# One step of a hybrid RG-LRU and GLA layer: smaller blocks in the order of the work, and a weight load in four pieces

## Chip, cores and metric

The kernel runs on one core of one Trainium2 chip. The metric is the device time of one execution in microseconds, lower being better. The core's engines each work through a queue of their own: TensorE (PE in the profile, with its weight loads as PEld), VectorE (DVE), ScalarE (ACT), GpSimd (POOL) and SyncE (SP), which here does little but issue DMA transfers. They wait for one another through semaphores, so an instruction that must wait holds up everything behind it on its engine.

## The reference

One layer of a decoder, for a prompt of 2048 tokens and 8 single-token samples, all in float32, width 1024:

```
ada = silu(c) @ w_ada + b_ada;  shift, scale, gate = split(ada)
hn = rmsnorm(x, g_norm) * (1 + scale) + shift
xa, za, q, k, v, glr, zg = split(hn @ w_in)
xc = conv_b + 4-tap causal conv of xa
gx, ga = sigmoid(xc @ w_gate_x + b), sigmoid(xc @ w_gate_a + b)   # 8 diagonal blocks of 128
log_a = 8 * ga * log_sigmoid(lambda);  a = exp(log_a)
h_t = a_t * h_{t-1} + sqrt(1 - exp(2 log_a)) * gx * xc;  y_lru = h * silu(za)
log_alpha = log_sigmoid(glr @ w_gla_g2 + b) / 16
S_t = diag(alpha_t) S_{t-1} + k_t^T v_t;  o_t = q_t S_t           # 4 heads, dk 128, dv 256
y_gla = rmsnorm(o) * g * silu(zg)
x = x + gate * (concat(y_lru, y_gla) @ w_out);  y = rmsnorm(x, g_final)
```

The outputs are y and the new states, for the prompt and for the samples.

## The kernel before, in words

**Precision and tiles.** Every float32 operand of a matmul is split into a high part (a rounded copy, made by ScalarE, `S.copy`) and a low part (what is left, by VectorE, `V.tensor_tensor(... subtract)`). A product is three matmuls, high by high, high by low and low by high, added in one PSUM bank. There are four banks tagged `acc`, two tagged `tp` (for turns, that is transposes through TensorE, and for some products), and one each tagged `kv` and `o`.

**Stages.** The prompt is worked in two halves of 1024 tokens. In each half come first the four GLA heads in the order 3, 0, 1, 2 (`gla_head`): projections of q, k and v (L396 to L398, L702 to L704), the decay (L852 to L866, L940 to L977), and the chunks of the linear attention (L1014 to L1053), whose output is turned and written to DRAM. Then come the `couples`: pairs of column blocks of the input projection for the RG-LRU and for zg, each by a Strassen-Winograd scheme of seven products (`Couple.product`, L1549) in place of eight. In the second half the split weights of these products are read back from DRAM (`wtd`), where the first half put them. The output projection follows, 16 `Pair`s of token tiles by the same scheme (L2117).

**What sets the order.** A function that is due later is put in a heap by `after(units, fn)`. `tick(0.5)` moves the clock after each half of a projection (24 matmuls, in bursts of three) and after each product of a couple (12 matmuls, 2.72 us in the chain of waits), and calls what has come due. So one unit is some 5.4 us. A scheduler then orders the instructions of each engine by readiness, but a block under `with behind(V)` is tied behind the last VectorE instruction written before it (L718), and so for S and SP.

**The pieces that the change touches.**

- `second_rows` (L1311 to L1352) makes the inputs of the second half during the first: `load` brings in two x tiles by SyncE (L1314), `norm` squares them on ScalarE (L228), `scale` takes the inverse root of the mean squares (`scales`, 12 small VectorE instructions, L163 to L169) and multiplies two tiles by it (`times`, L244), and `step` turns them (L255) in four steps, writing sums for the Winograd scheme with GpSimd (L1338 to L1342). The x buffers come free with the last turn.
- `sample_out` (to L1107) norms a head's output for the samples in the same way; its turn is L1131, and what it makes is added at L1134.
- `gla_turn` (L1109) turns a head's output of 512 tokens, 128 values at a time: four transposes into a `tp` bank (L1113), twice. `keep` copies the bank to `ob` (L1220, ScalarE) and stores that to `od` in DRAM (L1221, issued by ScalarE). `ob` has `half + 1` buffers: one in the first half. For the last head `gate` multiplies in place instead (L1227). `finish` (L1231) calls it.
- `out_weights(f, ...)` (L773) multiplies the output weights by the gate vector and makes their Winograd sums, a half of the rows in each of two calls, f=0 during the heads of the second half and f=1 during its couples. `begin(q)` loads the gate and its bias `bt` (L779, L780); `add` adds them (L785); `step` does one of four pairs of row tiles for each of two column halves: a product with the gate (L806), four differences (L810 to L813), a high and a low part (L828), stores to `wd` and `wd2`, and the load of the next tile (L795).
- `low_op(..., units)` (L1903) loads a token operand of the couples from `fd` (L1298) and splits it (`split_op`, L1305 and L1306) so many units later. S1 and S2 are two of these operands.
- `Couple.prepare` splits the weights of a product (L1495, L1496), and `combine` forms the weight sums (L1529 to L1531) on GpSimd. For the first four products of a half's first couple this happens at once (`now`); for others by `after`.
- `Lru.gates` (L1674) makes the two gate products of a 512-token segment: `xh`, `xl` are the high and low part of the convolution's output (L1671, L1672), `wgh`, `wgl` those of the gate weights. Two gates, each three matmuls in the order wgh xh, wgh xl, wgl xh (L1682 to L1684), then a tanh (L1685).
- The weights of the first output product, B11, are 2 MB, both parts already made (`wd2`). `early_w` loads them (L1924) in the last couples, at the product that the table `at` of the `couples` call names: (10, 0) is the first product of couple 10. `early_rows` (L1943) loads and splits the first token operands of the output projection in the same stretch.

## Time and profile before

| | |
|---|---|
| median of 3 runs | 1478.83 us (1476.04 to 1481.50) |
| the profiled execution | 1481.88 us, of which its span is 1480.1 us |
| mean granted TensorE clock | 0.988 |
| instructions in the span | 22516 |
| DMA, mean over the span | 231 GB/s |
| first half: heads, then couples | to about 343 us, to about 611 us |
| second half: heads, then couples | to about 893 us, to about 1148 us |
| output projection, and its end | to about 1466 us, to 1480 us |

Times inside the span are counted from its first instruction. A row of the timeline has the start, the duration, the engine, the line, the operation, what it writes and reads, and in brackets the idle time of the engine before it with what ended that. A row of a list of waits has who waited, for what, the total, how often, and the longest. The chain of waits follows the work that ended last back to its start. A queue's name with a q (SPq, ACTq) is an engine's instruction that issues a transfer or handles a semaphore. The granted clock is the share of TensorE's full clock that the chip allowed.

### The profile page before, as it was taken

To read this page: it belongs to the slowest core of one execution; us is meant where nothing else is said; L and a number is where in the kernel's file an instruction comes from. 1 tells how busy PE (TensorE), PEld (TensorE's weight loads), DVE (VectorE), ACT (ScalarE), POOL (GpSimd) and SP (SyncE) were. 2 spreads that over 40 slices of the span, in tenths; PEclk is the share of its full clock that TensorE was granted. 3 is DMA by queue.
4 is the path that set the end of the run, shared out by engine and by line. 5 is a ranking of instruction groups with operands and counts; after the bars stand their busy time and mean duration, and the time that the engine had idled before them with its cause. 6 is when DMAs were issued, how large, how long until landed. Compare 5 with 4: busy or idle time off the path is not lost.

```text
span 1480.1 us, 22516 instructions
## 1 busy us (share of the span) xinstructions
PE 1417.9 (96%) x8113; PEld 1172.7 (79%) x8113; DVE 1098.0 (74%) x2402; ACT 699.0 (47%) x1310; POOL 212.2 (14%) x258
## 2 busy tenths in 40 slices
PE   8999998899999999889899999999999999999997
PEld 6888978787777777779798888778777787777786
DVE  5767975658788888756767864788866886688886
ACT  4634353544675767333433532666563532144332
POOL 0200154334313222001111100000002000000000
PEclk9999999999999999999999999999999999999999
DMA  9725665536778558973857536798889867694352
GB/s 322 263 87 191 220 231 191 206 142 222 273 257 289 190 181 288 341 252 136 287 171 275 172 107 225 277 296 290 290 260 371 326 212 271 231 354 141 133 174 100
DMA packets 172436, 341.89 MB, mean 231 GB/s; under 512 B 12418, under 2 KB 101794, under 8 KB 168605
## 3 DMA queue, kind: packets, MB, share of 16 engines
q1 hardware_dynamic: 136325, 277.92, 55.1%
q0 software_dynamic: 13392, 46.54, 8.0%
q10 hardware_dynamic: 22608, 15.99, 3.3%
q8 instruction: 64, 1.05, 0.3%
q14 instruction: 47, 0.39, 0.1%
HBM read 205.78 MB, written 134.69 MB: 230 GB/s over the span
## 4 chain that ended last, share of the span: by engine, by line
PE 52%; DVE 15%; DMA 9%; ACT 5%; issue 4%; SPq 0%; ACTq 0%; DVEq 0%
PE acc L2117 11%; PE tp L2117 8%; PE acc L1549 6%; PE tp L1549 4%; PE acc L704 3%; PE acc L702 3%; PE acc L703 3%; DVE tg L1700 2%; PE acc L396 2%; PE acc L397 2%; PE acc L398 2%; DMA raw<-in_w_in_dram 1%; DVE op L1496 1%; DVE cv L1667 1%; DVE tx L1698 1%
## 5 line engine op out<-in xcount | busy, mean ns | idle before, releaser
L1549 PE MATMUL acc<-op,op 128*128 128x512 f32 x1056 | 252.3, 393 | 6.1 <-DMA op<-wtd 3.6
L1549 PEld LDWEIGHTS acc<-op,op 128*128 128x128 f32 x1056 | 198.2, 189 | 49.5 <-DMA op<-wtd 4.0
L1549 PE MATMUL tp<-op,op 128*128 128x512 f32 x792 | 196.1, 393 | 2.3 <-DVE acc L1559 2.3
L2117 PE MATMUL acc<-w,a 128*128 128x512 f32 (+1 forms) x792 | 187.2, 389 | 1.8 <-DVE w L1982 1.8
L2117 PEld LDWEIGHTS acc<-w,a 128*128 128x128 f32 x792 | 146.7, 188 | 37.6 <-issue 3.4
L1549 PEld LDWEIGHTS tp<-op,op 128*128 128x128 f32 x792 | 146.9, 188 | 34.4 <-DVE acc L1559 3.2
L396 PE MATMUL acc<-w,op 128*128 128x256 f32 (+1 forms) x508 | 151.9, 299 | 2.0 <-ACT w L374 1.2
L397 PE MATMUL acc<-w,op 128*128 128x256 f32 (+1 forms) x508 | 145.4, 286 | 0.4 <-DVE w L375 0.4
L398 PE MATMUL acc<-w,op 128*128 128x256 f32 (+1 forms) x508 | 145.5, 286 | 0.2 <-DVE op L271 0.2
L2117 PE MATMUL tp<-w,a 128*128 128x512 f32 x564 | 137.2, 393 | 0.0
L2117 PEld LDWEIGHTS tp<-w,a 128*128 128x128 f32 x564 | 105.2, 188 | 27.9 <-issue 5.2
L702 PE MATMUL acc<-op,w 128*128 128x512 f32 x296 | 121.9, 412 | 0.3 <-ACT w L374 0.3
L704 PE MATMUL acc<-op,w 128*128 128x512 f32 x296 | 117.0, 395 | 0.0
L703 PE MATMUL acc<-op,w 128*128 128x512 f32 x296 | 116.5, 394 | 0.0
L396 PEld LDWEIGHTS acc<-w,op 128*128 128x128 f32 x508 | 98.0, 193 | 4.2 <-ACT w L374 1.6
L397 PEld LDWEIGHTS acc<-w,op 128*128 128x128 f32 x508 | 97.3, 192 | 1.5 <-DVE w L375 0.6
L398 PEld LDWEIGHTS acc<-w,op 128*128 128x128 f32 x508 | 97.2, 191 | 0.6 <-DVE op L271 0.4
L1979 ACT CAST a<-s 128x512 fp32r<-128x512 f32 x61 | 36.5, 619 | 102.9 <-issue 35.6
L228 ACT ACTIVATE junk<-on 128x256 bf16<-128x256 f32 x64 | 26.7, 417 | 113.1 <-DVE on L1053 95.1
L1667 DVE SCALAR_TENSOR_TENSOR cv<-xa,vecT,cv 128x512 f32<-128x512 f32 x96 | 72.8, 758 | 5.8 <-ACT cv L1665 5.1
L1049 DVE TENSOR_TENSOR states<-states,pkv 128x256 f32<-128x256 f32 x60 | 25.0, 417 | 58.3 <-PE po L1048 58.0
L704 PEld LDWEIGHTS acc<-op,w 128*128 128x128 f32 x296 | 55.9, 189 | 12.2 <-DVE w L375 0.2
(442 smaller groups left out, 2833.3 us busy)
## 6 DMA issues: line engine op xcount, KB each, us to landing
wtd<-op SPq DMA_DIRECT2D x77, 512.0 KB
op<-wtd SPq DMA_DIRECT2D x77, 512.0 KB
w<-parts SPq DMA_DIRECT2D x16, 1024.0 KB
a<-mixd SPq DMA_DIRECT2D x63, 256.0 KB
parts<-w POOLq DMA_DIRECT2D x12, 1024.0 KB, 5.9
w<-wd SPq DMA_DIRECT2D x10, 1024.0 KB
wr<-in_w_in_dram SPq DMA_DIRECT2D x18, 512.0 KB
wada<-in_w_ada_dram SPq DMA_DIRECT2D x16, 512.0 KB
```

The lines of the kernel that those rows point to most:

```text
L228: S.activation(junk[:m, :n], x, AF.Square, accum_out=out)
L396: PE.matmul(ps, part(0, kt, c), hi[:, kt % 4], start=kt == 0, stop=False)
L397: PE.matmul(ps, part(0, kt, c), lo[:, kt % 4], start=False, stop=False)
L398: PE.matmul(ps, part(1, kt, c), hi[:, kt % 4], start=False, stop=kt == KT - 1)
L702: PE.matmul(ps[:, :n], hi[:, kt], a, start=kt == 0, stop=False)
L703: PE.matmul(ps[:, :n], hi[:, kt], b, start=False, stop=False)
L704: PE.matmul(ps[:, :n], lo[:, kt], a, start=False, stop=kt == KT - 1)
L1549: PE.matmul(ps, w[:, u, k], t[:, v, k], start=q < 3 and (k, u, v) == (0, 0, 0), stop=(k, u) == (3, 1), skip_group_check=True)
L1667: V.scalar_tensor_tensor(cv, xa[:, k:k + 512], cw[k], cv, op0=OP.mult, op1=OP.add)
L1700: V.tensor_tensor_scan(h, a, tx, 0.0 if self.half == 0 else hc[:, j:j + 1], op0=OP.mult, op1=OP.add)
L1979: S.copy(t[:, 0, k], (low(t) if src is None else src)[:, k])
L2117: PE.matmul(ps, t[:, u, k], w[:, v, k, c], start=(q < 3 or ps is own) and (k, u, v) == (0, 0, 0), stop=(k, u) == (3, 1), skip_group_check= ...
```

## The change

Eight edits, none of which changes a matmul's count:

1. `second_rows.scale` and `sample_out.scale` leave the inverse root to the scheduler; only the multiplication is tied behind VectorE, and in `second_rows` it comes half a unit later.
2. `gla_turn` takes a `gap`. For the first three heads of the first half the second turn comes one unit after the first.
3. The first couple's `combine` runs on VectorE instead of GpSimd. The later couples keep GpSimd.
4. The gate products are ordered wgh xh and wgl xh for both gates, then wgh xl for both with the tanh behind each. The two gates' banks are open together.
5. `out_weights(0)` begins after 2.5 units in place of 0.5, and its bias is added after 2 units in place of 1.5; for f=1 after 1 in place of 1.5.
6. The operands S1 and S2 of the second half are split 3 units after their load is issued, in place of 2.
7. B11's 2 MB load becomes four of 512 KB, a row tile each, behind the products (10, 0), (9, 5), (9, 6) and (10, 2). In the order of the products these come in turn.
8. `early_rows` loads its second operand a unit after the first and splits it 3.5 units in, in place of 3.

```diff
--- before.py
+++ after.py
@@ -785,7 +785,7 @@
                     V.tensor_tensor(g, g, bt, op=OP.add)
                 step(q, 0, r, g)

-            after(1.5, add)
+            after(2 - f, add)

         def load(q, m):
             r = hp.tile([P, 2, 2, 256], F32, tag="r", name="r", bufs=2)
@@ -1099,19 +1099,24 @@
         square_sum(xp, ss[:, :1], os_, P, DV)

         def scale():
+            rsqrt(gp, rs[:, :1], ss[:, :1], 1, P, 1.0 / DV)
             with behind(V):
-                rsqrt(gp, rs[:, :1], ss[:, :1], 1, P, 1.0 / DV)
                 V.tensor_scalar(os_, os_, rs[:, :1], None, op0=OP.mult)
         after(0.5, scale)
         after(2.5, done, True)
         more()

-    def gla_turn(h, s, on, done):
-        for dt in range(2):
+    def gla_turn(h, s, on, done, gap=0):
+        def one(dt):
             pt = tps()
             for c in range(4):
                 PE.transpose(pt[:, c * P:(c + 1) * P], on[:, c, dt * P:(dt + 1) * P], ident)
             done(2 * h + dt, dt, pt)
+        one(0)
+        if gap:
+            after(gap, lambda: one(1), True)
+        else:
+            one(1)

     def silu(z, src):
         log_exp[0] = False
@@ -1232,7 +1237,7 @@
             if final and (s, 1) not in zs:
                 after(0.5, lambda: finish(s), True)
                 return
-            gla_turn(h, s, prep[s, "run"][1], gate(s) if final else keep(s))
+            gla_turn(h, s, prep[s, "run"][1], gate(s) if final else keep(s), 0 if final or half else 1)

         pk = None
         if not wv:
@@ -1320,9 +1325,13 @@
             after(0.5, lambda: scale(p, x, ss))

         def scale(p, x, ss):
-            with behind(V):
-                times(x, scales(xp, ss, 2))
-            after(1, lambda: step(p, x, 0))
+            rs = scales(xp, ss, 2)
+
+            def mult():
+                with behind(V):
+                    times(x, rs)
+                after(1, lambda: step(p, x, 0))
+            after(0.5, mult)

         def step(p, x, k):
             if p == 0 and not ready:
@@ -1500,7 +1509,7 @@
             if q == B11:
                 self.slot(q)
                 split(q, b11)
-                (self.combine if now else lambda: after(self.wait, self.combine))()
+                (lambda: self.combine(V)) () if now else after(self.wait, self.combine)
             elif q == T2:
                 self.slot(q)
                 if now:
@@ -1515,7 +1524,7 @@
                 self.slot(q)
                 split(q, {B21: b21, T3: b12, B22: b22, T4: b11}[q])

-        def combine(self):
+        def combine(self, q=G):
             r = self.raw
             b11, b12, b21, b22 = [r[:, 4 * k:4 * k + 4, b] for k in range(2) for b in range(2)]
             if self.half == 0:
@@ -1526,9 +1535,9 @@
                 sample_cols(lambda kt: r[:, kt].rearrange("p b n -> p (b n)"), 2 * P,
                             [(zsam[:, n], 1.0) for n in self.sam], tmp, acc, self.wait)
             t = self.t2 = lp.tile([P, 4, P], F32, tag="t2", name="t2")
-            G.tensor_tensor(b11, b12, b11, op=OP.subtract)
-            G.tensor_tensor(t, b22, b11, op=OP.subtract)
-            G.tensor_tensor(b12, b22, b12, op=OP.subtract)
+            q.tensor_tensor(b11, b12, b11, op=OP.subtract)
+            q.tensor_tensor(t, b22, b11, op=OP.subtract)
+            q.tensor_tensor(b12, b22, b12, op=OP.subtract)

         keep, wait, more = None, 0.75, ()

@@ -1677,11 +1686,14 @@
                 self.tx, self.tg = self.t_("tx"), self.t_("tg")
             tx, tg = self.tx, self.tg
             c = slice(SEGS[s][0], SEGS[s][0] + 512)
+            both = []
             for g, (out, bias) in enumerate(((tx, hbx), (tg, hba))):
                 ps = gps()
+                both.append((ps, out, bias))
                 PE.matmul(ps, wgh[:, g], xh, start=True, stop=False)
-                PE.matmul(ps, wgh[:, g], xl, start=False, stop=False)
-                PE.matmul(ps, wgl[:, g], xh, start=False, stop=True)
+                PE.matmul(ps, wgl[:, g], xh, start=False, stop=False)
+            for g, (ps, out, bias) in enumerate(both):
+                PE.matmul(ps, wgh[:, g], xl, start=False, stop=True)
                 S.activation(out[:, c], ps, AF.Tanh, bias=bias[:, j:j + 1], scale=0.5)
             if s == 0:
                 return
@@ -1894,13 +1906,13 @@
     after(5, samples_silu)
     owp = gpx.enter_context(tc.tile_pool(name="owp", bufs=1, side="right"))
     ow = Scratch(6)
-    after(0.5, lambda: out_weights(0, ow, owp, lambda: ow.tile([P, 2, 256], F32, tag="g"), lambda: low_op(1, S1, fd[4], units=2)))
+    after(2.5, lambda: out_weights(0, ow, owp, lambda: ow.tile([P, 2, 256], F32, tag="g"), lambda: low_op(1, S1, fd[4], units=3)))
     scs.append(Scratch(3))
     log_exp[0] = False
     for k, h in enumerate(HEADS):
         w = gla_head(1, h, k, w=w)
         if k == 1:
-            low_op(1, S2, fd[5], units=2)
+            low_op(1, S2, fd[5], units=3)
     flush()
     samples_conv()
     gpx.close()
@@ -1925,10 +1937,11 @@
         else:
             SP.dma_start(low(w), wd[f, WD[q]])

-    def early_w(q, place):
+    def early_w(k):
         def load():
-            with behind(SP):
-                load_w(0, q, place)
+            if k == 0:
+                wts[0, B11] = ops.tile([P, 2, 4, 512], F32R, tag="o0", name="w")
+            low_dma(wts[0, B11][:, :, k].bitcast(F32), wd2[0, :, :, k])
         return load

     def open_pre():
@@ -1943,9 +1956,11 @@

         r = [lp.tile([P, TH], F32, tag=tag, name="r").rearrange("p (q k t) -> p q k t", q=2, k=4) for tag in ("tx", "a")]
         lo = [early[n][:, 1].bitcast(F32) for n in range(2)]
-        for n in range(2):
+        def load(n):
             low_dma(lo[n], mixd[2 * n, :, :4])
             low_dma(r[n], mixd[2 * n + 1, :, :8].rearrange("p (q k) t -> p q k t", q=2))
+        load(0)
+        after(1, lambda: load(1))

         def add(n):
             with behind(S), behind(V):
@@ -1961,7 +1976,7 @@
                 V.tensor_tensor(early[2 + n][:, 1], r[n][:, 0], early[2 + n][:, 0].bitcast(F32), op=OP.subtract)

         after(2, lambda: add(0))
-        after(3, lambda: add(1))
+        after(3.5, lambda: add(1))

     open_s()
     done = []
@@ -1969,7 +1984,7 @@
     end = Zg(1, HEADS[2])
     end.more = [lambda: am.rearrange("p c t -> p (c t)")]
     couples([Lru(1, j) for j in range(KT)] + [Zg(1, h) for h in HEADS[:2]] + [end], at={(0, 0): lambda: low_op(1, S4, fd[7]),
-                                                (0, 6): lambda: low_dma(o[4][0, 0, HEADS[3]], St[HEADS[3]]), (9, 2): open_pre, (10, 0): early_w(B11, 0)})
+                                                (0, 6): lambda: low_dma(o[4][0, 0, HEADS[3]], St[HEADS[3]]), (9, 2): open_pre, (10, 0): early_w(0), (9, 5): early_w(1), (9, 6): early_w(2), (10, 2): early_w(3)})
     flush()
     sx.close()
```

How the order moves is shown at three places. The first is VectorE at the start of the second half's first head. `L785` adds the bias; `L852` to `L854` split the decay's low-rank input `g`, `L866` copies its turn, `L910` is the low part of the values, `L884` copies the samples' values. Before:

```order
L910 TENSOR_TENSOR vl<-acc,vh 128x256
L785 TENSOR_TENSOR scratch<-scratch,bt 128x512
L884 COPY vs<-acc 8x68
L806 TENSOR_TENSOR scratch<-scratch 128x512
L884 COPY vs<-acc 8x68
L806 TENSOR_TENSOR scratch<-scratch 128x512
L852 CAST g_6513<-acc 8x16
L853 CAST g_6513<-acc 8x16
L854 TENSOR_TENSOR g_6513<-acc,g_6513 8x16
```

After, some twenty rows further on in the same queue:

```order
L866 CAST gls<-tp 48x512
L910 TENSOR_TENSOR vl<-acc,vh 128x256
L852 CAST g_6583<-acc 128x16
L853 CAST g_6583<-acc 128x16
L854 TENSOR_TENSOR g_6583<-acc,g_6583 128x16
L910 TENSOR_TENSOR vl<-acc,vh 128x256
L852 CAST g_6616<-acc 128x16
L853 CAST g_6616<-acc 128x16
L854 TENSOR_TENSOR g_6616<-acc,g_6616 128x16
L785 TENSOR_TENSOR scratch<-scratch,bt 128x512
L806 TENSOR_TENSOR scratch<-scratch 128x512 x2
L866 CAST gls<-tp 48x512
```

The add and the two products with the gate have moved from ahead of the samples' copies and the last five splits of g to behind them all, in front of the second large copy L866.

The second place is VectorE between the second and the third head of the second half, around the split of the operand S2 (`op_7653` before, `op_7640` after). `L1262` (L1267 after) finishes the scaled keys that TensorE turns at L1014; `L1018` masks the attention products. Before:

```order
L1306 TENSOR_TENSOR op_7653<-op_7653 128x1024
L168 SCALAR_TENSOR_TENSOR rs_t<-rs_t,rs_x 128x1
L951 TENSOR_TENSOR xb<-xb,e 128x8
L1306 TENSOR_TENSOR op_7653<-op_7653 128x1024
L169 SCALAR_TENSOR_TENSOR ors_7451<-rs_t,rs_y 128x1
L1271 TENSOR_TENSOR e<-acc,e 128x512
L1104 TENSOR_SCALAR os<-os,ors_7451 128x256
L1262 SCALAR_TENSOR_TENSOR xb<-acc,xb 128x512
L785 TENSOR_TENSOR scratch<-scratch,bt 128x512
```

After, where L1267 stands eleven rows ahead of the first of these:

```order
L1018 COPY_PREDICATED am<-mask,tp 128x512
L1024 TENSOR_TENSOR kTl<-tp,kTh 128x512
L1021 TENSOR_TENSOR aml<-am,amh 128x512
L1277 SCALAR_TENSOR_TENSOR xb<-acc,xb 128x512
L1139 SCALAR_TENSOR_TENSOR mixs<-tp,gsc,zsam 128x8 x2
L1049 TENSOR_TENSOR states<-states,pkv 128x256
L1053 COPY on<-po 128x256
L1050 TENSOR_SCALAR states<-states,f 128x256
L1049 TENSOR_TENSOR states<-states,pkv 128x256
L1053 COPY on<-po 128x256
L1050 TENSOR_SCALAR states<-states,f 128x256
L1311 TENSOR_TENSOR op_7640<-op_7640 128x1024 x2
```

The split (L1311 after) has moved from ahead of the keys to behind the mask and two state updates L1049.

The third place is TensorE among the last heads of the first half (near 290 us in the profile), at the turns of one head's output; `op_146`, `op_147` and so on are the token operands of a value projection that runs there. Before:

```order
L704 MATMUL acc<-op_146,w 128x512
L1113 MATMUL tp<-ident,on 128x128 x4
L702 MATMUL acc<-op_147,w 128x512
L703 MATMUL acc<-op_147,w 128x512
L1113 MATMUL tp<-ident,on 128x128 x4
L704 MATMUL acc<-op_147,w 128x512
```

After, the second of the two turns:

```order
L255 MATMUL tp<-ident,scratch 128x128 x4
L704 MATMUL acc<-op_148,w 128x512
L1113 MATMUL tp<-ident,on 128x128 x4
L702 MATMUL acc<-op_149,w 128x512
L703 MATMUL acc<-op_149,w 128x512
L1014 MATMUL tp<-xb,e 128x128 x4
L1017 MATMUL tp<-ident,e 128x128 x4
```

The first turn stays ahead of op_147; the second has moved thirteen matmuls of the projection further, to two matmuls ahead of the L1014 and L1017 that come next.

## The prediction

> **What bounds the kernel now.** I read the page's busy times first, then the list of what TensorE waited for.
>
> ```profile
> PE 1417.9 (96%) x8113; PEld 1172.7 (79%) x8113; DVE 1098.0 (74%) x2402; ACT 699.0 (47%) x1310; POOL 212.2 (14%) x258
> ```
>
> TensorE is busy for 1417.9 of the span's 1480.1 us, and no edit removes a matmul. All that can be won lies in the remaining 62 us and in stretches at a lower clock. The list of TensorE's waits (total, times, longest) names the idle time that the eight edits touch:
>
> ```profile
> PE tp L1014 <- DVE xb L1262: 5.3, 1, 5.3
> PE tp L255 <- DVE am L1018: 4.3, 1, 4.3
> PE tp L1014 <- ACT ob L1220: 3.7, 1, 3.7
> PE tp L864 <- DVE g L854: 3.6, 1, 3.6
> PE acc L1549 <- DMA op<-wtd: 3.6, 1, 3.6
> PE gps L1682 <- ACT xh L1671: 3.6, 5, 1.3
> PE gps L1683 <- DVE xa L1657: 2.7, 4, 0.7
> PE acc L1549 <- DVE op L1496: 2.5, 1, 2.5
> PE gps L1683 <- DVE xl L1672: 1.5, 3, 0.7
> PE tp L1131 <- DVE f L967: 0.9, 1, 0.9
> ```
>
> Five are single waits of 3.6 to 5.3 us. What follows each is in a table of stretches (length; busy time and count of PE, weight loads, DVE, ACT, POOL; granted clock; DMA share; GB/s):
>
> ```profile
> 228.00:232.00 4.00, 3.93 (x21) 3.93 (x22) 2.61 (x6) 1.77 (x4) 2.20 (x5) 0.57 0.71 281
> 290.00:297.00 7.00, 6.26 (x23) 5.58 (x24) 2.12 (x3) 3.89 (x7) 3.83 (x7) 0.51 0.32 115
> 349.00:356.00 7.00, 6.90 (x43) 4.95 (x44) 6.46 (x11) 2.87 (x4) 1.97 (x2) 1.00 0.95 358
> 635.00:642.00 7.00, 6.39 (x30) 6.31 (x31) 3.19 (x16) 0.98 (x3) 1.52 (x2) 0.53 0.70 166
> 734.00:738.00 4.00, 3.84 (x17) 3.69 (x18) 3.96 (x13) 0.81 (x2) 0.00 (x0) 0.60 0.03 12
> 1130.00:1135.00 5.00, 2.03 (x5) 1.65 (x6) 2.62 (x5) 0.71 (x2) 0.18 (x1) 0.81 1.03 409
> 1135.00:1140.00 5.00, 5.00 (x20) 4.01 (x20) 2.59 (x4) 0.59 (x1) 0.75 (x1) 0.85 1.06 422
> ```
>
> Behind each of the five the granted clock is low; behind the wait of 2.5 us (349) it is 1.00. The work lost is (1 - clock) times the busy time: 0.43 x 3.93 = 1.7 at 228, 0.49 x 6.26 = 3.1 at 290, 0.47 x 6.39 = 3.0 at 635, 0.40 x 3.84 = 1.5 at 734, and by the lengths 0.95 + 0.75 = 1.7 at 1130. So the five cost 20.5 us of idleness and 11 us of clock. A wait must only be made short enough to win the second part. [...]
>
> **Norm scales (228).** The wait is on L1018, and VectorE's queue shows why it came late, with ScalarE's square sum before it:
>
> ```profile
> 221.28 1.06 ACT L228 ACTIVATE junk<-scratch 128x1024 bf16<-128x1024 f32 x1 [1.60 <-DMA scratch<-in_x_prompt_dram]
> 222.46 0.17 DVE L163 TENSOR_SCALAR rs_x<-ss 128x2 f32<-128x2 f32 x1 [4.71 <-ACT junk L228]
> 224.84 1.41 DVE L244 TENSOR_SCALAR scratch<-scratch,rs 128x1024 f32<-128x1024 f32 x2
> ```
>
> The inverse root stood at the head of the queue until the x rows were squared, and L1018 behind the L244. These two now come after L1018, which saves 1.4 us for certain; the rest of 2.9 us is in the class that kept its clock, 3.1 in all. If x also lands earlier, all 4.3 + 1.7 = 6.0 goes: the transposes that free its buffers move up by several matmuls, in front of the small turns. Between 1.4 and 6.0 I take 4.5. The same unpinning of a sample's inverse root touches the 0.9 us at L1131: 0.6, between 0 and 0.9.
>
> **Second turned output (290).** ScalarE's rows, the store's issue and the copy that waited for it:
>
> ```profile
> 283.17 0.33 ACTq L1221 DMA_DIRECT2D od<-ob  x1
> 290.00 0.69 ACT L1220 ACTIVATE ob<-tp,gsc 128x512 f32<-128x512 f32 x1 [2.36 <-DMA od<-ob]
> ```
>
> The one ob buffer is stored from 283.17 to about 290.0, 6.8 us, and the second turn's PSUM bank waits for that. Moving the turn puts it two matmuls ahead of L1014 and L1017, and L1017 takes its bank. So a store as slow as this one leaves 3.7 less about 0.6 (the matmuls now in front of the wait): a gain of 0.6, or 3.7 with the clock kept. A store that lands 3 us sooner, since the 1 MB store of weight parts now goes out earlier, gives all 6.8. I take 4.5.
>
> **First couple's sums (349).** The seven-product weights are split on VectorE while GpSimd sums:
>
> ```profile
> L1496 DVE TENSOR_TENSOR op<-raw,op x6: 679/1668/1776, 342.8 to 349.6; 128x512 fp32r<-128x512 f32 x6
> 346.79 1.71 POOL L1530 TENSOR_TENSOR t<-raw 128x512 f32<-128x512 f32 x1
> 344.18 4.88 DVE op L1496 x3
> ```
>
> The first row's times are least, median and most: a split takes 1.67 us beside GpSimd and 0.68 alone. The last row, from the chain, is the three splits on the path. Three splits and three sums at 0.68 are 4.1, a gain of 0.8 if all sums come first; with the sums behind the splits it is the whole 2.5. I take 1.6. Nothing to lose is left on GpSimd, but VectorE gets 2 us more, so the low end is 0.
>
> **Gate products (409 to 957).** One wait from the timeline:
>
> ```profile
> 409.02 0.50 PE L1683 MATMUL gps<-xl,aml 128*128 128x512 f32 x1 [0.65 <-DVE xa L1657]
> 409.36 0.39 PE L1684 MATMUL gps<-xh,aml 128*128 128x512 f32 x1
> 409.59 0.39 PE L1682 MATMUL gps<-xh,aml 128*128 128x512 f32 x1
> ```
>
> The product with xl waits 0.65 us; matmuls start 0.23 us apart, so the three more of xh that now go before it cover 0.69. Both L1683 entries, 2.7 + 1.5 = 4.2, go. The wait for xh itself (3.6) stays. The first tanh comes 0.7 us later, while ScalarE is busy 47% of the span. I take 4.0, from 2.8 (a third left) to 4.2.
>
> **Output weights later (635 and 734).** SyncE's issue and VectorE's row behind it, for the bias and then for the operand, with one gap on VectorE:
>
> ```profile
> 622.21 0.41 SPq L780 DMA_DIRECT2D bt<-in_b_ada_dram  x1
> 632.44 0.69 DVE L785 TENSOR_TENSOR scratch<-scratch,bt 128x512 f32<-128x512 f32 x1 [4.54 <-DMA bt<-in_b_ada_dram]
> 633.29 1.67 SPq L887 DMA_DIRECT2D vsd<-vs  x4
> 651.81 0.68 DVE L866 CAST gls<-tp 48x512 fp32r<-48x512 f32 x1 [5.01 <-PE tp L864]
> 721.70 0.59 SPq L1298 DMA_DIRECT2D op<-fd  x1
> 728.90 1.04 ACT L1305 CAST op<-op 128x1024 fp32r<-128x1024 f32 x1 [6.88 <-DMA op<-fd]
> SPq L795 <- DMA wd<-scratch: 31.5, 3, 11.8
> ```
>
> The add of the bias blocked VectorE for 4.5 us, and L854 and the transpose L864 behind it. It now stands behind the last L854, in front of the L866 that had 5.0 us of idleness before it; its load is issued behind the sample rows' stores, some 10 us later, and with the same 10 us to land it is there when the add comes. Gain 3.6 + 3.0 = 6.6; a load 3 us late would eat the idleness and up to 3 of it. I take 6.2. The operand S2 took 7.2 us from issue to cast and then blocked L1262. With three units its split comes after L1018 and two state updates, so L1262 is free: 5.3 + 1.5 = 6.8. But its load now stands behind one more L795, and L795 waits for stores, 11.8 us at most (last row). If it lands as late as that, the split blocks the next L1049, and nothing is won. Between 0 and 6.8 I take 5.0.
>
> In the second half's couples the add comes half a unit, some 2.7 us, earlier; TensorE waited for none of these, and I cost it at nothing; the cover is the load's lead, and gone it costs at most those 2.7 us.
>
> **First output weight (1133).** SyncE's issue, two pieces of the chain and a later wait:
>
> ```profile
> 1118.56 0.32 SPq L1924 DMA_DIRECT2D w<-wd  x1
> 1118.92 14.01 DMA op<-wtd
> 1148.30 9.60 DMA w<-wd
> 1167.32 1.43 PE L2117 MATMUL acc<-w,a 128*128 128x512 f32 x5 [1.79 <-DVE w L1982]
> ```
>
> The 2 MB load was issued 0.4 us ahead of a 512 KB operand, which took 14.0 us. At the 409 to 422 GB/s of the stretches above, 2 MB take 5.1 us and a quarter 1.3, so the operand comes 3.8 us sooner, and 3.6 + 1.7 = 5.3 go. The same stretches have a DMA share of 1.03 to 1.06, though: what goes later pushes something else, the next weight's 9.6 us or the wait of 1.8 at 1167. Between 0 and 5.3 I take 3.8. [...]
>
> **The sum.** 4.5 + 0.6 + 4.5 + 1.6 + 4.0 + 6.2 + 5.0 + 3.8 = 30.2 us. An order that changes on every engine makes waits of its own; I take one of the size of 2.5 and one of 0.7 from the list, 3.2. The net is 27.0. The profiled execution took 1481.88 us, so 1454.9 for such a one; it lies 3.05 above the median of the runs, 1478.83, and against that I predict 1451.8, written as 1452.
>
> **Rivals.** *Two waits move on.* The ob store stays slow and L1017 waits (0.6 in place of 4.5), and S2's load lands late behind L795 (0 in place of 5.0). For it: both causes, the single buffer and the store wait of L795, are still there. Against it: both places get more time. Net 27.0 - 8.9 = 18.1, so 1460.7.
>
> *The DMA engines bound the end of the couples.* The four pieces give the same bytes to engines that were full; the wait at 1133 goes to a later weight and the one of 1.8 doubles. Net 27.0 - 3.8 - 1.8 = 21.4, so 1457.4.
>
> *VectorE is blocked by the output weights* (the other side). From the second half's first head on, eight steps (two column halves of four) stand at fixed places in VectorE's queue. They now start two units later, beside the heads' decays, and L806 in each waits for a load that can be held up by 11.8 us of stores. A step that blocks as L785 did costs 3.6 + 3.0 = 6.6. Four such steps take back the 27: 1478.8 - 27.0 + 26.4 = 1478.2, no change. From six on it is slower: 1478.8 - 27.0 + 39.6 = 1491.4. For it: one of the eight did this before. Against it: the other steps cost TensorE nothing in the list, and S2's wait was a load's and not theirs.
>
> *The change does not do what it says.* The instructions of the small turns, the splits and the bias stand elsewhere in the queues, so this can only hold for the scales, where L163 is still ahead of L1018; that is the 1.4 above.
>
> **Chances.** Forecast 0.58; two waits move on 0.18; DMA bound 0.12; together 0.88 for faster. Four blocked steps 0.08, six 0.04. Half a per cent is 7.4 us, about what a measurement of this kernel tells from no change, since its three runs spread over 5.5. All high ends together (6.0 + 0.9 + 6.8 + 2.5 + 4.2 + 6.6 + 6.8 + 5.3 = 39.1, no new wait) give 1439.7, all low ends (1.4 + 0 + 0.6 + 0 + 2.8 + 3.6 + 0 + 0 = 8.4, less 3.2) 1473.6; neither is likely in every step at once. The range of 1443 to 1466 holds the forecast with some 9 us to the low side and both faster rivals with 5 us above the first; it leaves out the two blocked cases and some of the mixed ones.
>
> **What would show it.** Right: no entry of TensorE's waits over 3 us, the stretches at 0.5 clock gone from the five places, L1696 without a wait on xl, the two L244 starting after L1018, L785 without idleness ahead of it, and the first operand load after the first quarter landing in under 10 us. Each of my steps is wrong where its wait is still there under the new line, above all L1017 on ob, L1049 behind S2's split, and L1549 on op. The prediction as a whole is wrong if TensorE's idle time and its half-clock time together fall by under 15 us, or if a new wait of over 3.5 us stands in the second half's heads.

## The result and the profile after

The changed kernel takes 1465.7 us (median of 11 runs, 1462.78 to 1473.13) beside 1480.48 us for the kernel before (11 runs). The ratio is 0.9914, with a 95% interval of 0.9895 to 0.9933. That is 0.9% faster, clear of the half per cent. It is 14.8 us by the medians, 12.7 by the ratio, where 27 were forecast. The profiled execution took 1465.7 us with a span of 1463.9.

Lines that the change shifted have new numbers: L1693 to L1697 are the gates (L1682 to L1685 before), L1558 the couples' products (L1549), L2132 the output products (L2117), L1504 and L1505 the weights' split (L1495, L1496), L1680 the copy xh (L1671), L1311 the split of an operand (L1306), L1343 the scaled turn in `second_rows` (L1334), L1225 the copy to ob (L1220). The edits of an experiment can shift them again by a few lines.

TensorE's row of the page, and what it waited for (total, times, longest):

```profile
PE 1417.0 (97%) x8113; PEld 1172.2 (80%) x8113; DVE 1096.9 (75%) x2405; ACT 697.1 (48%) x1310; POOL 205.3 (14%) x255
```

```profile
PE gps L1693 <- ACT xh L1680: 6.8, 4, 3.8
PE acc L310 <- ACT am L305: 3.9, 2, 2.2
PE po L1091 <- DVE on L1053: 3.2, 1, 3.2
PE acc L1558 <- ACT op L1504: 2.8, 1, 2.8
PE tp L1558 <- DVE acc L1568: 2.4, 1, 2.4
PE acc L2132 <- DVE w L1997: 2.0, 2, 1.8
PE pkv L1042 <- DVE kTl L1024: 2.0, 2, 1.2
PE acc L304 <- DVE tp L1564: 1.2, 1, 1.2
PE tp L1136 <- ACT p L820: 0.6, 1, 0.6
```

All of the five long waits of before are gone, and so are those on xl and on the first couple's splits; of the sample turn's 0.9, 0.6 is left. The eight entries of the prediction's list that were to go (all but the one on xh and the sample's) came to 27.2 us. Yet TensorE's idle time, the span less its busy time, fell only from 62.2 to 46.9 us, by 15.3. The other 11.9 are what came back: waits that are new or grew, less some small ones that shrank. The list above shows them: on xh now 6.8 instead of 3.6, on the copy L305 of the samples' columns 3.9 instead of 0.4, on L1053 behind the split of S2, on ScalarE's copies in front of the first product.

The clock gave little. In the two profiled executions the mean granted clock is 0.988, before as after, and TensorE's busy time fell by 0.9 us. Over all runs the clock is 0.987 for the changed kernel (11 runs) and 0.986 for the kernel before (the 49 runs beside the experiments); that is some 3 us of lost clock less, an estimate from one less the clock, times the span. Between 100 and 1440 us the changed kernel's stretches at half clock lasted 3.41 us each. These are stretches of that length, in pairs (length; busy time and count of PE, weight loads, DVE, ACT, POOL; granted clock; DMA share; GB/s):

```profile
330.80:334.21 3.41, 0.79 (x3) 0.35 (x3) 0.87 (x2) 2.52 (x5) 2.81 (x6) 1.00 0.73 261
334.21:337.62 3.41, 3.41 (x8) 2.73 (x9) 3.41 (x5) 1.55 (x4) 3.22 (x5) 0.50 0.74 299
409.31:412.72 3.41, 1.22 (x7) 0.70 (x5) 1.79 (x4) 3.38 (x6) 1.35 (x2) 1.00 0.42 171
412.72:416.13 3.41, 3.41 (x11) 2.83 (x12) 3.41 (x5) 0.80 (x2) 0.00 (x0) 0.50 0.25 77
443.44:446.85 3.41, 2.31 (x9) 1.25 (x8) 3.41 (x7) 0.00 (x0) 0.00 (x0) 1.00 0.06 17
446.85:450.26 3.41, 2.46 (x13) 2.12 (x14) 3.41 (x8) 2.88 (x6) 0.00 (x0) 1.00 1.12 370
1146.59:1150.00 3.41, 1.42 (x5) 0.65 (x4) 3.41 (x7) 3.41 (x8) 0.00 (x0) 1.00 1.01 428
1150.00:1153.41 3.41, 3.41 (x9) 2.65 (x9) 3.41 (x7) 1.03 (x2) 0.00 (x0) 0.50 1.02 403
```

Behind the three stretches in which TensorE was busy for only 0.79, 1.22 and 1.42 us the clock was 0.50 for 3.41 us. Around the wait of 1.75 us near 447 TensorE was busy for 2.31 and 2.46 us, and the clock stayed at 1.00. Counting 3.41 us at a clock of 0.50 as one half-clock window, there are seven in the changed kernel between 100 and 1440 us, and there were seven before (those after 290 and 635 were double, 6.83 us each). Five of the seven lie behind waits that are new or grew, each only 1.7 to 3.8 us. The other two lie behind waits that stood before the change too, on L1568 (now 2.4 us, at 594) and at the output's first products (1.8 us, at 1150); the clock behind them was 1.00 then. Before, the first of them read

```profile
PE tp L1549 <- DVE acc L1559: 2.3, 2, 2.1
```

So that the two counts are equal is in part luck.

Taken together, 27.2 us of waits went, and 11 us of clock were to go with the five long ones: 38.2. The span fell by 16.2. So 22.0 us came back, 11.9 as idle time and some 10 as clock.

### The profile page after: what moved, and what is told of

It is laid out like the page before. It is cut to its first block, busy times and chain, and to the rows that moved or that the text cites. A ratio compares the mean times of both kernels' runs of the same rounds, so it can differ in the third digit from the quotient of the medians.

```text
span 1463.9 us, 22541 instructions
## 1 busy us (share of the span) xinstructions
PE 1417.0 (97%) x8113; PEld 1172.2 (80%) x8113; DVE 1096.9 (75%) x2405; ACT 697.1 (48%) x1310; POOL 205.3 (14%) x255
## 4 chain that ended last, share of the span: by engine, by line
PE 64%; DVE 12%; DMA 8%; ACT 7%; issue 6%; POOL 1%; SPq 1%; ACTq 0%; DVEq 0%; POOLq 0%
PE acc L2132 11%; PE tp L2132 8%; PE acc L1558 8%; PE tp L1558 7%; PE acc L397 3%; PE acc L396 3%; PE acc L398 3%; PE acc L702 3%; PE acc L704 3%; PE acc L703 3%; DVE cv L1676 2%; DVE tg L1712 2%; PE po L1048 1%; DMA wada<-in_w_ada_dram 1%; DMA op<-fd 1%
## 5 line engine op out<-in xcount | busy, mean ns | idle before, releaser
L1558 PE MATMUL acc<-op,op 128*128 128x512 f32 x1056 | 252.2, 393 | 3.1 <-ACT op L1504 2.8
L1558 PEld LDWEIGHTS acc<-op,op 128*128 128x128 f32 x1056 | 198.5, 189 | 45.9 <-ACT op L1504 3.3
L1558 PE MATMUL tp<-op,op 128*128 128x512 f32 x792 | 201.1, 401 | 2.4 <-DVE acc L1568 2.4
L2132 PE MATMUL acc<-w,a 128*128 128x512 f32 (+1 forms) x792 | 189.3, 392 | 2.8 <-DVE w L1997 2.0
L1558 PEld LDWEIGHTS tp<-op,op 128*128 128x128 f32 x792 | 150.7, 193 | 36.4 <-DVE acc L1568 3.4
L2132 PEld LDWEIGHTS acc<-w,a 128*128 128x128 f32 x792 | 147.9, 189 | 39.8 <-issue 3.4
L2132 PE MATMUL tp<-w,a 128*128 128x512 f32 x564 | 137.2, 393 | 0.0
L2132 PEld LDWEIGHTS tp<-w,a 128*128 128x128 f32 x564 | 105.2, 188 | 27.9 <-issue 5.2
L396 PEld LDWEIGHTS acc<-w,op 128*128 128x128 f32 x508 | 96.2, 190 | 3.3 <-ACT w L374 1.6
L397 PEld LDWEIGHTS acc<-w,op 128*128 128x128 f32 x508 | 95.6, 188 | 1.6 <-DVE w L375 0.6
L398 PEld LDWEIGHTS acc<-w,op 128*128 128x128 f32 x508 | 95.7, 188 | 0.6 <-DVE op L271 0.4
L1049 DVE TENSOR_TENSOR states<-states,pkv 128x256 f32<-128x256 f32 x60 | 25.1, 418 | 54.6 <-PE po L1048 54.3
```

What stands on the lines that cost most here:

```text
L396: PE.matmul(ps, part(0, kt, c), hi[:, kt % 4], start=kt == 0, stop=False)
L397: PE.matmul(ps, part(0, kt, c), lo[:, kt % 4], start=False, stop=False)
L398: PE.matmul(ps, part(1, kt, c), hi[:, kt % 4], start=False, stop=kt == KT - 1)
L1558: PE.matmul(ps, w[:, u, k], t[:, v, k], start=q < 3 and (k, u, v) == (0, 0, 0), stop=(k, u) == (3, 1), skip_group_check=True)
L2132: PE.matmul(ps, t[:, u, k], w[:, v, k, c], start=(q < 3 or ps is own) and (k, u, v) == (0, 0, 0), stop=(k, u) == (3, 1), skip_group_check= ...
```

## The experiments

The idle time below is the span less TensorE's busy time in the profiled execution; half-clock windows are those between 100 and 1440 us. Ratios are to the kernel before on the same chip; the kernel before had medians of 1479.4 to 1480.8 in all of them. The idle time and the windows are those of a single execution each; the times are medians. Theory in short: each new wait has a cause at its place, and taking that away takes the wait away. Rival: any other order makes other waits of about the same sum.

| run | us | ratio (95% interval) | idle | half-clock windows |
|---|---|---|---|---|
| before | 1480.5 | | 62.2 | 7 |
| after | 1465.7 | 0.9914 (0.9895 to 0.9933) | 46.9 | 7 |
| e1 rows on time | 1467.9 | 0.9919 (0.9896 to 0.9942) | 50.1 | 8 |
| e2 S2 tied | 1461.9 | 0.9882 (0.9861 to 0.9902) | 43.9 | 8 |
| e3 gates old | 1464.5 | 0.9892 (0.9866 to 0.9917) | 50.5 | 5 |
| e4 f=1 add old | 1465.8 | 0.9900 (0.9870 to 0.9930) | 49.5 | 7 |
| e5 output weights only | 1469.7 | 0.9927 (0.9905 to 0.9949) | 56.9 | 4 |
| e6 first weight whole | 1468.5 | 0.9928 (0.9901 to 0.9955) | 49.8 | 6 |
| e7 turns together | 1475.4 | 0.9971 (0.9956 to 0.9987) | 57.1 | 10 |
| e8 sums on GpSimd | 1473.8 | 0.9958 (0.9942 to 0.9974) | 54.3 | 10 |
| e9 S2 tied, gates old | 1460.7 | 0.9865 (0.9837 to 0.9893) | 45.9 | 3 |
| e10 S2 tied, gate by gate | 1457.1 | 0.9845 (0.9817 to 0.9873) | 44.6 | 1 |
| e11 e10 and rows on time | 1459.9 | 0.9858 (0.9829 to 0.9886) | 41.7 | 4 |
| e12 e9 and f=1 add old | 1456.8 | 0.9841 (0.9811 to 0.9870) | 44.8 | 4 |
| e13 e10 and f=1 add old | 1458.7 | 0.9856 (0.9834 to 0.9877) | 43.4 | 3 |
| e14 gap only | 1472.5 | 0.9946 (0.9928 to 0.9965) | 54.3 | 8 |

**e1: the second half's rows on time** (from the changed kernel)

```diff
                     times(x, rs)
-                after(1, lambda: step(p, x, 0))
+                after(0.5, lambda: step(p, x, 0))
```

> The changed kernel, but the turns of the second half's inputs come half a unit after the scaling instead of one, so that the four rounds end as early as before the change. Theory (each new wait has a local cause): the wait of 2.8 us of the first product (L1558 on ACT op) at 333 comes from L1343, which is late by four times half a unit, two units or 11 us, and holds up ScalarE in front of the first couple's copies; it falls under 1 us, with it the half-clock window behind it, and the time falls by 2.8 + 1.7 = 4.5 us. Rival (any new order makes waits of the same total somewhere): the total idle time of TensorE stays at 47 us within 2 us, whatever happens at this place, and the time stays within 2 us of 1465.7.

What it was to mend, on ScalarE in the changed kernel, ahead of the first couple's copies:

```profile
331.69 0.56 ACT L1343 ACTIVATE scratch<-tp,Sh,Gm 128x256 f32<-128x256 f32 x1 [2.82 <-DMA fd<-scratch]
332.70 0.60 ACT L1504 CAST op<-raw 128x512 fp32r<-128x512 f32 x1
```

And TensorE's waits in e1:

```profile
PE acc L310 <- ACT am L305: 5.4, 3, 2.2
PE po L1091 <- DVE on L1053: 4.3, 1, 4.3
PE tp L1014 <- ACT scratch L1343: 1.4, 1, 1.4
```

The wait at the first product is gone from the list, so its cause was that lag. But the wait on L1053 is 4.3 instead of 3.2, a third one on L305 came, and one of 1.4 on the earlier turns. The idle time is 50.1, three more than without the edit, and the time is the same. At its place the theory held; the gain of 4.5 us did not come. That the edit itself moved the waits, as the rival says, is not shown: the wait on L1053 is 2.8 to 4.7 us in the eight profiles that keep the edit to S2, and the third one on L305 (1.5 us, near 560) stands in five of the seven with the new gate order and not in two, the changed kernel among them.

**e2: S2's split tied later** (from the changed kernel)

```diff
-            low_op(1, S2, fd[5], units=3)
+            with behind(SP):
+                s2_split = load_op(1, S2, fd[5])
+
+            def s2_tied():
+                with behind(S), behind(V):
+                    s2_split()
+            after(7, s2_tied)
```

> The changed kernel, but the operand S2 is split seven units after its load's issue and tied behind VectorE there, some 35 us later in the queue. Theory (local causes): the wait of L1091 on L1053 (3.2 us) at 733 goes, with its half-clock window, and the time falls by 3.2 + 1.7 = 4.9 us; nothing new comes, since the operand is first needed more than 100 us later. Rival (any order makes waits): a wait of 2 us or more comes within 60 us behind that place and the time stays within 2 us of 1465.7.

The place in the changed kernel, SyncE's issue and the cast and split that waited for it:

```profile
715.85 1.36 SPq L795 DMA_DIRECT2D scratch<-in_w_out_dram  x2
719.82 0.84 SPq L1303 DMA_DIRECT2D op<-fd  x1
728.98 1.05 ACT L1310 CAST op<-op 128x1024 fp32r<-128x1024 f32 x1 [8.27 <-DMA op<-fd]
730.06 2.57 DVE L1311 TENSOR_TENSOR op<-op 128x1024 fp32r<-128x1024 f32 x2 [5.66 <-ACT op L1310]
732.88 0.42 DVE L1053 COPY on<-po 128x256 f32<-128x256 f32 x1
```

The load goes out four microseconds behind L795, which had waited 9.2 us for stores; it takes 9.2 us, and the split holds up L1053 behind it. In e2 the split runs at 774.6 us with no wait, no entry for L1091 is left, and nothing of 2 us or more comes in its place before 830 (0.95 at 768, the sample's turn, as before the change). The time is 3.8 us under the changed kernel (4.7 by the ratios), of 4.9 expected; the intervals of the ratios overlap a little. That this split makes the wait is shown. The edit moves the split and ties the load at once, so it does not tell how much of it the late load makes.

**e3: the gates' old order** (from the changed kernel)

```diff
                 PE.matmul(ps, wgh[:, g], xh, start=True, stop=False)
-                PE.matmul(ps, wgl[:, g], xh, start=False, stop=False)
-            for g, (ps, out, bias) in enumerate(both):
-                PE.matmul(ps, wgh[:, g], xl, start=False, stop=True)
+                PE.matmul(ps, wgh[:, g], xl, start=False, stop=False)
+                PE.matmul(ps, wgl[:, g], xh, start=False, stop=True)
                 S.activation(out[:, c], ps, AF.Tanh, bias=bias[:, j:j + 1], scale=0.5)
```

> The changed kernel with the gate products in the old order. Theory (local causes): the old waits on xl come back, seven of 0.65 us or 4.2 in all; and if the waits of L310 on the copy L305 (2.2 and 1.8 us at 412 and 448) are made by the first tanh coming later on ScalarE, they go, so that the edit as a whole won nothing: time within 2 us of 1465.7. Rival (the L305 waits have nothing to do with the gates): they stay and the time rises by 4 us.

TensorE's waits on xl in e3:

```profile
PE gps L1692 <- DVE xa L1666: 2.8, 4, 0.7
PE gps L1692 <- DVE xl L1681: 1.5, 3, 0.6
```

The 4.3 us on xl are back, and of the two waits on L305 0.2 us is left. The time is 1.2 us lower, within the noise. The edit that I priced at 4.0 us won nothing: it exchanged seven short waits, of 0.7 us at most, with no half-clock window behind them in the kernel before, for two of 2 us, one of which has such a window behind it (412.72).

That the gate order makes these two waits is shown; the expected way, through a later tanh, holds for the first. ScalarE's rows in the changed kernel, a tanh and the two copies L305 with the stores ahead of the second:

```profile
402.81 0.68 ACT L1697 ACTIVATE tx<-gps,hbx 128x512 f32<-128x512 f32 x1
412.12 0.36 ACT L305 COPY am<-acc 128x256 f32<-128x256 f32 x1
445.73 1.61 ACTq L712 DMA_DIRECT2D mixd<-zs  x3
447.38 0.37 ACT L305 COPY am<-acc 128x256 f32<-128x256 f32 x1 [4.68 <-DVE zs L1627]
```

The gate products of this tanh end at 399.5, 3.3 us ahead of it: on ScalarE it now stands behind a cast that waits for a load. The activations that follow from it, with two table loads of 1.28 us, stand ahead of the first copy. In e3 the tanh starts at 402.13, as its products end (402.2). The second copy stands behind three stores (L712) for which ScalarE waited 4.7 us on VectorE; in e3 it stands ahead of them, at 440.48. There the order of the queue changed, and no late tanh is ahead of it.

**e4: the add in the second half's couples as before** (from the changed kernel)

```diff
-            after(2 - f, add)
+            after(2 - 0.5 * f, add)
```

> The changed kernel, but in the second half's couples the bias of the output weights is added after 1.5 units as before the change, not 1. Theory (local cause): the wait of L1693 on xh (3.8 us) at 1012 comes from L806 and L828 lying between the scan and the convolution on VectorE there; moved by half a unit it falls under 1.5, with its half-clock window, and the time falls by 2.3 + 1.7 = 4 us. Rival: the place is set by the scan L1712 (2.3 us) and the gates' bank alone; the wait stays over 3 and the time within 2 us of 1465.7.

```profile
PE gps L1693 <- ACT xh L1680: 5.8, 6, 2.3
```

The longest wait on xh falls from 3.8 to 2.3 (and stands at 1040 instead of 1012), as the theory had it, but two more came and the time did not move. With the interval of 0.987 to 0.993 a gain of 4 us can't be excluded either. Inconclusive on the time, so it was tried again in e12 and e13.

**e5: the output weights' edits alone** (from the kernel before)

```diff
-            after(1.5, add)
+            after(2 - 0.5 * f, add)
...
-    after(0.5, lambda: out_weights(0, ow, owp, lambda: ow.tile([P, 2, 256], F32, tag="g"), lambda: low_op(1, S1, fd[4], units=2)))
+    after(2.5, lambda: out_weights(0, ow, owp, lambda: ow.tile([P, 2, 256], F32, tag="g"), lambda: low_op(1, S1, fd[4], units=3)))
...
-            low_op(1, S2, fd[5], units=2)
+            low_op(1, S2, fd[5], units=3)
```

> The kernel before with the later output weights alone (f=0 begins after 2.5 units and adds after 2; S1 and S2 are split after 3 units; f=1 as before). Theory (local causes): the waits of 3.6 at 635 and 5.3 at 734 go with three half-clock windows (5.1 us of work), and the wait of L1091 on L1053 comes (3.2 + 1.7), as in the changed kernel: 14.0 - 4.9 = 9.1 us faster than before, that is 60% of the whole change's 14.8. Rival (waits come back wherever the order changes): under 4 us faster.

```profile
PE acc L1549 <- DMA op<-wtd: 4.5, 1, 4.5
PE tp L1014 <- ACT ob L1220: 3.7, 1, 3.7
PE tp L255 <- DVE am L1018: 3.3, 1, 3.3
PE po L1091 <- DVE on L1053: 3.0, 1, 3.0
PE acc L1549 <- DVE op L1496: 2.5, 1, 2.5
```

10.4 us faster than before, of 9.1 expected. The waits of 3.6 at L864 and 5.3 on L1262 are gone, the one on L1053 has come with 3.0, and the other long ones stand, with sizes up to 1 us apart. That is 70% of the 14.8 us of the whole change.

**e6: the first output weight whole** (from the changed kernel; `early_rows` loads and adds as before too)

```diff
-(10, 0): early_w(0), (9, 5): early_w(1), (9, 6): early_w(2), (10, 2): early_w(3)})
+(10, 0): early_w(B11, 0)})
```

> The changed kernel with B11 loaded in one piece of 2 MB and the first operands of the output projection loaded together as before. Theory (local cause): the wait of L1558 on op of 3.6 us comes back near 1118, with its half-clock window, and the time rises by 5.3 us to 1471. Rival (the DMA engines bound the end of the couples): a later wait shrinks by as much, and the time rises by under 2.

```profile
PE acc L1558 <- DMA op<-wtd: 5.4, 1, 5.4
```

The wait on op is back, longer than before the change, with two half-clock windows. The wait of 1.8 at the output's first products (L2132 on L1997) is not there, and the time rises by 2.8 us, or 2.1 by the ratios, not by 5.3; the intervals overlap, so even the rise is not clear of the noise. The theory holds at its place. That the gain is given back some 30 us later, as the rival had it, is only half shown: before the change, with the weight whole too, both waits stood.

**e7: both turns together** (from the changed kernel)

```diff
-            gla_turn(h, s, prep[s, "run"][1], gate(s) if final else keep(s), 0 if final or half else 1)
+            gla_turn(h, s, prep[s, "run"][1], gate(s) if final else keep(s), 0)
```

> The changed kernel with both turns of a head's output together, as before (no gap). Theory (local cause): the wait of L1014 on the ob copy comes back near 285, 3.7 us with one or two half-clock windows, and the time rises by 5.4 to 7.1 us, to 1471 or more. Rival (the store was slow only because the store of weight parts was in front of it, and that has moved for another reason): the wait stays under 1 us and the time within 2 us of 1465.7.

```profile
PE po L1091 <- DVE on L1053: 4.0, 1, 4.0
PE pkv L1042 <- DVE kTl L1024: 3.7, 2, 2.8
PE tp L255 <- DVE mixs L312: 2.3, 2, 1.3
```

The time rises by 9.7 us (8.4 by the ratios), but not by the wait that was expected: on the ob copy there is 0.8 us, not 3.7. The waits on L1018's follower L1024 and on the samples' turn L312 are what came back, with two double half-clock windows at 227 and 278. Both theories missed, the first in the cause, the rival in the time.

**e8: the sums on GpSimd** (from the changed kernel)

```diff
-                (lambda: self.combine(V)) () if now else after(self.wait, self.combine)
+                self.combine() if now else after(self.wait, self.combine)
```

> The changed kernel with the first couple's sums on GpSimd again. Theory (the wait there is now set by ScalarE's copies, late behind the turns of the second half's inputs): the first product still waits for ScalarE as long, and the second or third product waits for VectorE's splits at most 1 us more; time within 2 us of 1465.7. Rival (the sums' engine decides): the wait on VectorE of 2.5 us comes on top and the time rises by 2.5 to 4.2 us.

```profile
PE po L1091 <- DVE on L1053: 4.7, 1, 4.7
PE acc L1558 <- ACT op L1504: 3.5, 2, 2.0
PE tp L1558 <- ACT op L1504: 1.5, 1, 1.5
```

The time rises by 8.1 us (6.5 by the ratios). The first couple waits twice more, 1.5 us each, for copies that wait for the sums; with the first wait that is three half-clock windows there instead of one. My theory of no difference fell, and the rival's 2.5 to 4.2 was too small. The wait on L1053 also differs (4.7), 400 us later, where nothing was edited. Its size follows no edit in these profiles (see e1), so that share I can't explain.

**e9 to e13: what adds up.** e9 is e2's and e3's edits together, and e10 has, in place of the old gate order, each gate by itself with the high part first:

```diff
                 PE.matmul(ps, wgh[:, g], xh, start=True, stop=False)
                 PE.matmul(ps, wgl[:, g], xh, start=False, stop=False)
                 PE.matmul(ps, wgh[:, g], xl, start=False, stop=True)
                 S.activation(out[:, c], ps, AF.Tanh, bias=bias[:, j:j + 1], scale=0.5)
```

e11 is e10 with e1's edit, e12 is e9 with e4's, e13 is e10 with e4's.

> The changed kernel with S2's split tied seven units on and the gate products in the old order. Theory (local causes add up): the waits of 3.2 at 733, 2.2 and 1.8 at 412 and 448 go and two of 0.7 on xl come, 5.7 us of idleness less than the changed kernel, and two or three half-clock windows fewer: 8 to 10 us, 1456 to 1458. Rival (they do not add): no better than the tied split alone, 1461.9.

> As the one before, but each gate's products in the order wgh xh, wgl xh, wgh xl with its tanh right behind, so that the product with xl has 0.46 us of cover instead of 0.23 and the first tanh is late by nothing. Theory: the waits on L305 stay away as with the old order and the two on xl shrink to 0.5; 0.5 us better than the one before. Rival (any delay of the xl product's place brings the L305 waits back): they are there with 2.2 and 1.8.

> As the one before, and the turns of the second half's inputs half a unit after the scaling. Theory (local causes): the wait of 2 to 2.8 us at the first product (333) goes without a new one and the time falls by a further 2 to 4 us, to 1452 to 1455. Rival (that edit moves waits, as when it was made alone): the total idle time stays within 1 us and the time too.

> The tied split and the old gate order, and the bias of the output weights in the second half's couples added after 1.5 units as before the change. Theory (local cause): the wait of L1693 on xh at 1012 (3.8) falls to 2.3 or less, as when this was done alone, and the time falls by 1.5 to 3.2 us against the kernel without it. Rival (noise): no difference over 1 us.

> The tied split, each gate's products in the order wgh xh, wgl xh, wgh xl, and the bias of the output weights in the second half's couples added after 1.5 units. Theory (local causes add up): the wait on xh at 1005 (3.6 us) falls to 1.3 and moves to 1050 as it did with the old gate order, no wait on L305 and none over 0.6 on xl is left, and the time is 2 to 3 us under that with the earlier add, 1457.1: 1454 to 1455. Rival (the difference at this place is noise): within 1 us of 1457.

TensorE's waits in e10, those on xh, on xl and at the first product:

```profile
PE gps L1691 <- ACT xh L1680: 5.5, 4, 3.6
PE gps L1693 <- DVE xa L1666: 1.8, 4, 0.5
PE acc L1558 <- ACT op L1504: 1.7, 1, 1.7
```

No wait on L305 over 0.2 is left, and those on xl are 0.5 at most: with 0.46 us of other work ahead of it (the cover), the sum on xl falls from the 4.3 us of the old order to 2.6, and no tanh is delayed. The time is 3.6 us under e9, of 0.5 expected, with intervals that overlap. e9's 1460.7 lies between the theory's 1456 to 1458 and the rival's 1461.9. e11 shows again that the rows on time win nothing in time, although its idle time of 41.7 is the least of all. In e13 the wait on xh fell to 1.2, as in e12 (1.3), but e10, e12 and e13 lie at 1457.1, 1456.8 and 1458.7 with intervals that overlap. So the earlier add makes that wait, and it is not worth more than the noise. e10 and e12 beat the changed kernel by 8.6 and 8.9 us, by the ratios 0.9845 and 0.9841 against 0.9914, with intervals that do not meet that of the changed kernel. Idle time is the smaller part of that, 2.3 and 2.1 us in the profiles; the granted clock over the runs is 0.991 for e10 and 0.992 for e12, beside 0.987 for the changed kernel, by the estimate above some 5 and 7 us.

**e14: the gap alone** (from the kernel before: `gla_turn` and its call as in the change)

> The kernel before with the turn's gap alone (second turned output a unit later in the first three heads of the first half). Theory A (the ob store was the cost): only the wait of L1014 on the ob copy (3.7 us at 290) and its two half-clock windows change; 3.7 + 3.4 = 7.1 us faster than before at most, and the wait of L255 on L1018 at 228 stays at 4. Theory B (the turn stands in front of the x rows' last turns and delays everything behind): the wait at 228 falls by 1 us or more too, and the small waits of 0.7 to 1.0 us on L312 at 203 to 277 go; 8 to 11 us faster. Rival (with the rest of the old order the wait only moves): under 3 us faster.

TensorE's waits, then from ScalarE the store of one ob copy and the copy behind it, and from VectorE the inverse root of the x rows that stood ahead of L1018:

```profile
PE tp L1014 <- DVE xb L1267: 5.8, 1, 5.8
PE acc L1554 <- DMA op<-wtd: 5.0, 1, 5.0
PE tp L255 <- DVE am L1018: 1.6, 1, 1.6
```

```profile
276.70 0.33 ACTq L1226 DMA_DIRECT2D od<-ob  x1
283.19 0.69 ACT L1225 ACTIVATE ob<-tp,gsc 128x512 f32<-128x512 f32 x1 [0.66 <-DMA od<-ob]
217.71 0.33 DVE L163 TENSOR_SCALAR rs_x<-ss 128x2 f32<-128x2 f32 x1 [1.91 <-ACT junk L228]
```

7.1 us faster than before (8.0 by the ratio). The wait at 228 falls from 4.3 to 1.6 and the one of 1.0 on L312 goes: theory B holds in its waits. The time alone, 7 to 8 us, does not tell it from theory A. The inverse root starts at 217.71 us in place of 222.46, because the last turn of the older x rows comes at 206.8 instead of 211.6 and the load into their buffers goes out at 207.4 instead of 212.1. The store is about as slow as before, 6.5 us from issue to the copy behind it, and yet TensorE waits only 0.7 us for it. Two waits further on grew at the same time, 5.3 to 5.8 and 3.6 to 5.0.

## Why the prediction was wrong

Its sign, its list of waits and the places of the edits were right; its size was about twice too large. Point by point:

- **The step that failed** is the sentence that takes 3.2 us for new waits, one of 2.5 and one of 0.7. In its place the runs show 11.9 us of idle time and with it some 10 of clock, 22.0 in all. With it fell "A wait must only be made short enough to win the second part": behind the changed kernel's wait of 1.7 us at 546 (L1693 on xh) the clock was 0.50 for 3.41 us, from 549.25. The 11 us of clock were counted into the terms, and seven half-clock windows became seven others.
- **The terms do not add up.** The output weights alone (e5, 10.4 us) and the gap alone (e14, 7.1) make 17.5, more than all eight edits together. Of my signs, the scaled L244 now behind L1018, the add L785 without idleness ahead of it and the gates without a wait on xl came true; "no entry over 3 us" did not (3.8 and 3.2). A fall of idle and half-clock time by under 15 us was to show the whole wrong; it was 15.3 from idle time alone, so that sign was too lax.
- **Two waits move on**, the first rival, was right for S2: 3.2 us at L1091, made by a split that stands ahead of L1053 and whose load had waited behind L795. e2 shows the split's part; without it the time is 3.8 us lower. For the ob copy the rival was wrong.
- **Second turned output** (4.5). Worth 7.1 alone. The store stayed slow; the place was right, the reason too small: the moved turn also let the x rows' last turns forward, which took 2.7 us off the wait at 228 (e14). I had put that under the norm scales.
- **Norm scales** (4.5 and 0.6). The wait at 228 went, to 1.2 at L1024. How much of that is the scales' own, beside the gap's, was not tried alone. The sample's wait fell by 0.3, of 0.6. Their later multiplication cost something that I had not looked at: each of four rounds ends half a unit later, and the last ran into the first couple (e1). The unit count of a step that is moved must be followed to its end.
- **First couple's sums** (1.6). Too small: taking it back costs 6.5 to 8 us, of which its own waits explain 3.0 and two more half-clock windows 3.4. Yet in the changed kernel the place won nothing: the 2.5 us on VectorE went, and 2.8 on ScalarE's copies came, from the late turns (e1).
- **Gates** (4.0). Wrong in kind. The waits on xl went, and two on the copies L305 took their place (e3), one behind the later tanhs on ScalarE, one behind stores. I had said that ScalarE is busy 47% of the span; a share of the span says nothing of the stretch ahead of one copy.
- **Output weights** (6.2 and 5.0, so 11.2). 10.4 alone, near the sum but not by its parts, so in part luck. The bias's wait of 3.6 went with two half-clock windows, 7.0 in all, a little over the 6.2. S2's part took only 2.3 off the wait (5.3 to 3.0) and kept its half-clock window, half of the 5.0. The last 1.1 us are not traced.
- **First output weight** (3.8). 2.1 to 2.8, not clear of the noise: the wait goes. The wait of 1.8 at the output stays as it was, with a half-clock window behind it now; the DMA rival's doubling did not come.
- **The earlier add for f=1** (0). It makes the longest wait of the changed kernel, on xh, 3.8 us where 1.3 was (e4 2.3, e12 1.3 and e13 1.2 without it). That is the 2.7 that I had named as the most and left out of the sum; in the time it stays within the noise.

## What to carry to other kernels

When an engine is 96% busy, price each wait together with what the reordering itself makes: here 11.9 of the 27.2 us of waits that went came back and, in the two profiles, most of their clock. Follow a step that is moved by half a unit to the end of its chain, and each instruction that it passes on every queue. Tie work that has slack of 100 us far behind its load rather than one unit, and prefer cover that delays nobody (three products of one gate, high part first) to more cover that does.

## What the runs showed of the hardware

In the changed kernel's profile, between 100 and 1440 us, the granted clock is 1.00 except for seven stretches of 3.41 us at 0.50. They start at 334.21, 412.72, 549.25, 593.62, 733.58, 1013.47 and 1150.00. In the 3.41 us ahead of each TensorE was busy for 0.79, 1.22, 1.75, 1.46, 0.23, 1.02 and 1.42 us. In the kernel before, three such stretches lasted 3.41 us and two 6.83, from 290.0 and 634.8; in the first 3.41 us of these two TensorE was busy for 2.68 and 2.56 us. Around the wait of 2.5 us at 349, before the change, the clock stayed at 1.00:

```profile
344.64:348.05 3.41, 1.96 (x9) 1.25 (x7) 3.41 (x3) 1.81 (x4) 3.33 (x3) 1.00 0.72 202
348.05:351.47 3.42, 2.37 (x12) 2.06 (x13) 3.42 (x6) 2.06 (x4) 2.06 (x2) 1.00 0.99 371
```

From that I took it that a wait short enough keeps the clock; the runs do not show such a rule. The wait of 1.8 us at the output's first products shows both outcomes. Before the change TensorE was busy for 1.70 us in the stretch that holds it, and the clock stayed at 1.00, also in the 3.41 us that follow:

```profile
1163.83:1167.24 3.41, 1.70 (x7) 0.92 (x5) 3.41 (x7) 3.41 (x8) 0.00 (x0) 1.00 1.03 435
```

After it, TensorE was busy for 1.42 us in the stretch from 1146.59, and the clock was 0.50 in the next. So the same wait cost 1.8 us before and some 3.5 after, an estimate from its length and half of 3.41 us. The 1.70 us lie below the 1.75 ahead of 549.25, where the clock fell, so that such a busy time does not by itself tell the two cases apart; what does was not shown. The changed kernel's 11 runs spread over 10 us, and part of that goes with the clock: the longest, 1473.13 us, has the lowest, 0.985, and the shortest, 1462.78, the highest, 0.990. That is some 7 us of clock, by the estimate used above.
